# Residual stream kept with features on partitions, weights stationary in the two inner down projections, token factors by a product with ones

## The chip, the core and the metric

The kernel runs on one core of a Trainium2 chip. Its time is the device time of one execution in microseconds, the median of three runs. A profile of one more execution shows what each engine did: PE is TensorE (PEld its weight loads), DVE is VectorE, ACT is ScalarE, POOL is GpSimd, SP issues most of the transfers.

## What is computed

One decoder block on 256 tokens of 1024 features, in float32: a gated feed-forward part (FFN1), a mixing part with attention and a gated spatial branch side by side, a second feed-forward part (FFN2) and a last norm.

```python
h = h + 0.5 * swiglu(rmsnorm(h, ffn1_norm), w_gate, w_up, w_down)      # D_FF = 2816
n = rmsnorm(h, mix_norm)
z = n @ w_in                                   # q, k, v, u, gv
...
merged = gates[..., :D] * (attn @ w_branch_attn) + gates[..., D:] * (gm @ w_branch_gmlp)
h = h + merged @ w_out
h = h + 0.5 * swiglu(rmsnorm(h, ffn2_norm), ...)
return rmsnorm(h, final_norm)
```

`rmsnorm(x, g)` is `x * rsqrt(mean(x*x) + eps) * g`. The factor `rsqrt(...)` is one number for each token. It commutes with a projection, so the kernel projects `h * g` and multiplies the result by the token factor afterwards.

## The kernel before

**Products.** Every float32 operand is split into a high part, rounded to the format that TensorE takes in one pass, and a low part, the rest. A product is high·high + high·low + low·high. `by_passes` does it with the weights stationary and both parts of the activations side by side as the moving operand: one product of 512 columns (`mm_high`) and one of 256 (`mm_low`) for each block of 128x128 weights. `mm3` does it with the activations stationary and 512 columns of weights moving, in three products.

**Weights.** A unit is a piece of a weight matrix, 1 MB. It is fetched in two halves by SP's queue into seven buffers (`fetch_to`) and split in two halves into a ring of four tiles (`split_to`): ScalarE casts the high part, VectorE subtracts to get the low part, 128x1024 each. `unit(i, ahead)` splits two or three units ahead of the one that TensorE takes.

**Residual.** `h` has tokens on partitions (two groups of 128 tokens, 1024 features each). FFN1 and FFN2 have 22 blocks of 128 hidden features each. `products` makes gate and up of a block with weights stationary, `collect` adds the two halves of a PSUM bank (ScalarE copies one, VectorE adds), and `gate_up` multiplies by `rows` (the token factors, spread over all partitions by `rows_of`, which is two transposes on TensorE and a copy), then silu, a product and a split into `aT`.

`down` is the down projection with activations stationary, used three times: after FFN1 (22 blocks of 128 rows), as the output projection of the mixing part (8 blocks) and after FFN2 (22). After the first two, `done` multiplies by the norm's gain and sums the squares (`square_sum` on ScalarE, with a running sum, then `rstd_of`: two small VectorE operations and a power on GpSimd), and `put_T` turns the result by TensorE transposes, four to a bank, into `nT` with features on partitions for the next projection. The transposes stand among the products of the last two units. In FFN2 the first two blocks are made with the activations stationary (`by_tokens`) and turned afterwards.

**Order.** TensorE and SP take their instructions in the order of the code. The order on VectorE and ScalarE is a scheduler's, made when the program is built; each engine takes its list strictly in turn. PSUM has eight banks, given out in rotation.

Of the kernel before, what the change touches and what calls it, by code (L numbers as in the profile page):

```python
# [18 lines left out]
P = 128  # L19
# [24 lines left out]
def block_kernel(ctx, tc, t, out):  # L44
# [8 lines left out]
    psum = ctx.enter_context(tc.tile_pool(name="psum", bufs=8, space=PSUM))  # L53

# [4 lines left out]
    h = act.tile([P, NT, D], F32, tag="h", name="h")  # L59

    def norm_gain(ap, name):
        gb = consts.tile([P, ap.shape[-1]], F32, tag="gain", name=name)
        nc.sync.dma_start(gb, ap.to_broadcast([P, ap.shape[-1]]))
        return gb
# [4 lines left out]
    front = act.tile([P, FB * S], F32, tag="aTh", name="front")  # L69
    back = act.tile([P, ROW], F32, tag="nC", name="back")  # L70

    def load_front(queue, k, end, c0=0, c1=ROW):

        a, b = KB * (k + c0 > 0) + k * ROW + c0, KB + (end - 1) * ROW + c1
        to = back[:, c0:c1] if k == KB - 1 else front[:, a:b]
        queue.dma_start(to, t["first"][:, a:b])
# [10 lines left out]
    nc.vector.memset(eps, EPS)  # L87

# [33 lines left out]
    fetched, done_to = [2 * FIRST], [FIRST]  # L122
# [18 lines left out]

    def split_to(n):
        while done_to[0] < min(n, len(units)):
            i = done_to[0]
            done_to[0] += 1
            unit_tile(i)
            for hf in range(2):
                fetch_to(2 * i + hf + RAW)
                w, sl = parts[i], half(i, hf)
                split(w[:, sl, 0, :], w[:, sl, 1, :], raws.pop((i, hf)))  # L150
        fetch_to(2 * done_to[0] + RAW)
# [16 lines left out]
    def by_passes(sides, ks=range(KB)):  # L168


        for k in ks:
            if k < KB - 1:
# [7 lines left out]
        if KB - 1 in ks:  # L180
            for ps, of in sides:
                (sh, _), both = of(KB - 1)
                mm_high(ps, sh, both, False, True)
# [26 lines left out]
    def split(hi, lo, src):  # L210
        nc.scalar.copy(hi, src)  # L211
        nc.vector.tensor_sub(lo, src, hi.bitcast(F32))  # L212
# [19 lines left out]
    def gained(hh, gain, j, half):  # L232
        sl = slice(half * 512, half * 512 + 512)
        hg = tmp.tile([P, 512], F32, tag="hg", name=f"hg{j}{half}")
        nc.vector.tensor_mul(hg, hh[:, j, sl], gain[:, sl])
        return hg

    sums = {}

    def square_sum(hh, j, hf, name):  # L240

        if hf == 0:
            sums[name, j] = small.tile([P, 2], F32, tag="ss", name=f"ss{name}{j}")
        sq = tmp.tile([P, 512], BF16, tag="sq", name=f"sq{name}{j}{hf}", bufs=1)
        nc.scalar.activation(sq, hh[:, j, hf * 512:(hf + 1) * 512], AF.Square,
                             accum_out=sums[name, j][:, hf:hf + 1])

    def rstd_of(j, name):

        ss = sums.pop((name, j))  # L250
        ms = small.tile([P, 1], F32, tag="ms", name=f"ms{name}{j}")
        nc.vector.tensor_add(ms, ss[:, 0:1], ss[:, 1:2])
        nc.vector.tensor_scalar(ms, ms, 1.0 / D, EPS, op0=ALU.mult, op1=ALU.add)
        r = small.tile([P, 1], F32, tag="rstd", name=f"rstd{name}{j}")
        nc.gpsimd.tensor_tensor(r, ms, nhalf, op=ALU.pow)
        return r
# [20 lines left out]
    def by_tokens(name, i, nT, j):  # L277

        ps, w = bank(name), unit(i)
        tk = slice(j * P, (j + 1) * P)  # L280
        by_passes([(ps, lambda k: (tuple(p[:, tk] for p in block_of(nT, k)), w[:, k]))])
        return ps

    HALVES = ((0, 512), (512, 512))

    def down(i0, n_units, part_of, scale, hh, name, done, put=None, following=(), cuts=(HALVES, HALVES)):


# [28 lines left out]
        for j in range(NT):  # L317
            for hf, (c0, n) in enumerate(cuts[j]):
# [7 lines left out]
                if put and j == 1:  # L326
                    if hf == 0:
                        put(0, 0)
                        put(0, 1)
                    else:  # L330
                        for q in range(2):
                            put(1, q)
                            following[q]()

    def ffn_alloc(name):
        aT = (act.tile([P, FB, S], F32R, tag="aTh", name=f"{name}h"),
              act.tile([P, FB, S], F32R, tag="aTl", name=f"{name}l"))
        return aT, lambda k: (aT[0][:, k, :], aT[1][:, k, :])

    def gate_up(aT, gu, rows, name, f):  # L340
# [6 lines left out]
        split(aT[0][:, f, :], aT[1][:, f, :], a)  # L347

    def products(i0, nT, name, f):
        gu = tmp.tile([P, 2, S], F32, tag="gu", name=f"gu{name}{f}")  # L350
# [14 lines left out]
    def in_front(k, end):  # L365
        if k == KB - 1:
            return back.rearrange("p (k c) -> p k c", k=1)
# [4 lines left out]
    for k, end in zip(CUTS, CUTS[1:]):  # L372
# [24 lines left out]
        with tc.manual_schedule(engines={mybir.EngineType.DVE, mybir.EngineType.Activation}):  # L397
# [6 lines left out]
    fetch_to(2 * FIRST + RAW)  # L404
    for j in range(NT):
        nc.sync.dma_start(h[:, j, :], t["x"][j * P:(j + 1) * P, :])
    aT, aT_block = ffn_alloc("f1")
    first = act.tile([P, 4, 2, S], F32, tag="nD", name="first")
    rs = []
    for group in ((0, 1), (2,), (3,)):  # L410
        if group == (3,):
            for j in range(NT):
                for hf in range(2):
                    square_sum(h, j, hf, "1")
                rs.append(rstd_of(j, "1"))
# [11 lines left out]
    gu4 = products(f1, nT, "f1", 4)  # L427
    rows = rows_of(rs, "1")
# [23 lines left out]
    rs2 = {}  # L452

    def to_norm(nT, gain, rs, name):

        hg = {}

        def done(new, j, hf):
            hg[j, hf] = gained(new, gain, j, hf)
            square_sum(new, j, hf, name)  # L460
            if hf:
                rs[j] = rstd_of(j, name)

        return done, lambda j, hf: put_T(nT, hg.pop((j, hf)), j, hf)

# [3 lines left out]
    def value(ps, i0, j, u):  # L469
# [11 lines left out]
    gain3 = norm_gain(t["ffn2_norm"], "gain3")  # L481


    mix_a = act.tile([P, FB, S], F32, tag="aTh", name="mix_a")
# [312 lines left out]
```

## Time and profile before

| what | value |
|---|---|
| median of three runs | 538.65 us (538.56 to 539.09) |
| the profiled execution, device time | 538.97 us |
| its span (first to last instruction) | 537.2 us, so 1.8 us lie around it |
| TensorE busy | 529.5 us (99%) |
| VectorE, ScalarE busy | 389.8 us (73%), 300.3 us (56%) |
| GpSimd busy | 10.9 us (2%) |
| bytes moved | 103.02 MB, 192 GB/s on average |

The profiled execution is 0.3 us above the median. A busy TensorE is not TensorE at its peak: a product's shown duration overlaps the next one's, so costs are read from the distance between starts.

### The profile page before, as it was taken

Reading aid. Unit: us, or ns where it says so; the run is one execution under the profiler, and the core shown is the slowest. Engines: PE = TensorE matmul, PEld = TensorE weight load, DVE = VectorE, ACT = ScalarE, POOL = GpSimd, SP = SyncE. Lnnn points to the kernel's source line nnn. Section 1 sums busy time; section 2 is a strip of 40 time slices with the busy share of each in tenths; the row PEclk is TensorE's granted clock in tenths of the full one; section 3 lists DMA queues with packets and bytes.
Section 4 is the critical chain, followed back from the end, with each engine's and each line's share of the span. In section 5 each row is a group of like instructions: output and inputs, shape, how many; then the busy total and the mean of one; then the engine's idle time right before and its main releaser. Section 6 shows DMA issues by size and latency. Waiting matters only on the chain.

```text
span 537.2 us, 7918 instructions
## 1 busy us (share of the span) xinstructions
PE 529.5 (99%) x2962; PEld 459.7 (86%) x2962; DVE 389.8 (73%) x627; ACT 300.3 (56%) x534; POOL 10.9 (2%) x23
## 2 busy tenths in 40 slices
PE   8999999999999999999999999999999999999995
PEld 7888888888888888888888998888888888888884
DVE  6879988787534676968897786787787877854325
ACT  7877565565434356457886445675655656553302
POOL 0000000000000010000000000000000000000002
PEclk9999999999999999999999999999999999999998
DMA  8985765657755468564256545476546556565002
GB/s 312 418 297 187 249 220 169 210 173 246 244 196 194 159 204 266 171 212 145 84 190 201 172 140 198 141 231 221 207 164 207 181 188 204 168 206 186 30 0 78
DMA packets 29429, 103.02 MB, mean 192 GB/s; under 512 B 3408, under 2 KB 3920, under 8 KB 29392
## 3 DMA queue, kind: packets, MB, share of 16 engines
q1 hardware_dynamic: 29104, 102.20, 56.2%
q8 instruction: 23, 0.38, 0.3%
q10 hardware_dynamic: 288, 0.33, 0.2%
q14 instruction: 14, 0.11, 0.1%
HBM read 101.46 MB, written 1.05 MB: 191 GB/s over the span
## 4 chain that ended last, share of the span: by engine, by line
PE 97%; DMA 1%; DVE 0%; issue 0%; ACT 0%; POOLq 0%; DVEq 0%; POOL 0%; ACTq 0%
PE acch L199 9%; PE acch L197 9%; PE acch L198 9%; PE f2u L161 7%; PE f2g L161 7%; PE f1u L161 6%; PE f1g L161 6%; PE pgate L161 6%; PE f L161 4%; PE f2u L166 4%; PE f2g L166 4%; PE f1u L166 3%; PE f1g L166 3%; PE pgate L166 3%; PE pq L161 3%; PE f L166 2%
## 5 line engine op out<-in xcount | busy, mean ns | idle before, releaser
L212 DVE TENSOR_TENSOR w<-raw,w 128x1024 fp32r<-128x1024 f32 x180 | 217.4, 1224 | 61.2 <-ACT w L211 60.7
L211 ACT CAST w<-raw 128x1024 fp32r<-128x1024 f32 x180 | 181.7, 1056 | 68.6 <-PE acch L199 37.8
L161 PE MATMUL f2g<-n,w 128*128 128x512 f32 x160 | 62.7, 392 | 0.0
L161 PE MATMUL f2u<-n,w 128*128 128x512 f32 x160 | 62.6, 391 | 0.0
L161 PE MATMUL f1g<-n,w 128*128 128x512 f32 x144 | 56.3, 391 | 0.0
L161 PE MATMUL f1u<-n,w 128*128 128x512 f32 x144 | 56.3, 391 | 0.0
L166 PE MATMUL f2u<-n,w 128*128 128x256 f32 x160 | 39.2, 283 | 0.0
L166 PE MATMUL f2g<-n,w 128*128 128x256 f32 x160 | 39.1, 282 | 0.0
L166 PE MATMUL f1u<-n,w 128*128 128x256 f32 x144 | 35.3, 283 | 0.0
L166 PE MATMUL f1g<-n,w 128*128 128x256 f32 x144 | 35.2, 282 | 0.0
L161 PEld LDWEIGHTS f2u<-n,w 128*128 128x128 f32 x160 | 30.1, 188 | 5.7
L161 PEld LDWEIGHTS f2g<-n,w 128*128 128x128 f32 x160 | 30.1, 188 | 5.6
L197 PE MATMUL acch<-w,f1h 128*128 128x512 f32 x88 | 34.3, 390 | 0.0
L199 PE MATMUL acch<-w,f1l 128*128 128x512 f32 x88 | 34.3, 389 | 0.0
L198 PE MATMUL acch<-w,f1h 128*128 128x512 f32 x88 | 34.2, 389 | 0.0
L161 PE MATMUL pgate<-n,w 128*128 128x512 f32 x128 | 33.1, 395 | 0.0
L198 PE MATMUL acch<-w,f2h 128*128 128x512 f32 x84 | 32.7, 389 | 0.0
L199 PE MATMUL acch<-w,f2l 128*128 128x512 f32 x84 | 32.7, 389 | 0.0
L197 PE MATMUL acch<-w,f2h 128*128 128x512 f32 x84 | 32.7, 389 | 0.0
L161 PEld LDWEIGHTS f1u<-n,w 128*128 128x128 f32 x144 | 27.1, 188 | 5.1
L161 PEld LDWEIGHTS f1g<-n,w 128*128 128x128 f32 x144 | 27.1, 188 | 5.0
L166 PEld LDWEIGHTS f2u<-n,w 128*128 128x128 f32 x160 | 30.6, 191 | 0.8
(200 smaller groups left out, 992.8 us busy)
## 6 DMA issues: line engine op xcount, KB each, us to landing
raw<-in_f SPq DMA_DIRECT2D x84, 512.0 KB, 4.8
raw<-in_f1d SPq DMA_DIRECT2D x22, 512.0 KB, 4.3
raw<-in_f2d SPq DMA_DIRECT2D x22, 512.0 KB, 4.3
raw<-in_gate SPq DMA_DIRECT2D x16, 512.0 KB, 4.4
raw<-in_qk SPq DMA_DIRECT2D x8, 512.0 KB, 4.7
raw<-in_out SPq DMA_DIRECT2D x8, 512.0 KB, 4.4
front<-in_first SPq DMA_DIRECT2D x6, 384.0 KB, 6.5
raw<-in_v SPq DMA_DIRECT2D x4, 512.0 KB, 4.5
```

What stands on the lines that cost most here:

```text
L161: nc.tensor.matmul(ps, st, both.rearrange("p two n -> p (two n)"), start=first, stop=last)
L166: nc.tensor.matmul(ps[:, n:], st, both[:, 0, :], start=False, stop=False)
L197: nc.tensor.matmul(ps, sh, mh, start=first, stop=False)
L198: nc.tensor.matmul(ps, sh, ml, start=False, stop=False)
L199: nc.tensor.matmul(ps, sl, mh, start=False, stop=last)
L211: nc.scalar.copy(hi, src)
L212: nc.vector.tensor_sub(lo, src, hi.bitcast(F32))
```

## The change

`h` gets features on partitions. The two inner down projections become `down_features`: weights stationary, the hidden activations moving, one PSUM bank for each of eight blocks of 128 output features, so that the result is already turned and `put_T` is gone. Each finished bank is added to `h` by VectorE in two halves, ScalarE makes the high part with the gain as scale, and VectorE makes the low part one block later. Sums of squares are made across partitions: ScalarE squares (`square`), three adds fold eight blocks into one (`token_sums`; on GpSimd for the first norm, on VectorE for the others), the sum is split, and one product with a matrix of ones adds over partitions (`token_factors`). Four reducing operations against the identity then pick the two columns of sums out of PSUM, and GpSimd takes the power. `rows_of` for the first norm comes one block of FFN1 later, after block 5 in place of block 4. `in_order` fixes the order on VectorE and ScalarE to that of the code in three places; elsewhere it is the scheduler's still. The features are permuted in blocks of 32, and VectorE transposes of 32x32 with a trip through DRAM (`hd`, written at block 5 of FFN2 and read back at block 9 as `ht`) give the last down projection its tokens on partitions; that projection is as before. Gains come as columns. FFN2's first blocks use `products` like the others.

```diff
+    h = act.tile([P, KB, S], F32, tag="h", name="h")
...
+    def split_half(later=False):
+
+        i, hf = divmod(done_to[0], 2)
+        if hf == 0:
+            unit_tile(i)
+        fetch_to(done_to[0] + RAW)
+        done_to[0] += 1
+        w, sl = parts[i], half(i, hf)
+        return split(w[:, sl, 0, :], w[:, sl, 1, :], raws.pop((i, hf)), later)
...
-    def put_T(nT, src, j, half):
-
-        ps = bank(f"tr{j}{half}")
-        for b in range(4):
-            nc.tensor.transpose(ps[:, b * P:(b + 1) * P], src[:, b * P:(b + 1) * P], ident)
-        tk = slice(j * P, (j + 1) * P)
-        split(nT[half][:, :, 0, tk], nT[half][:, :, 1, tk], ps.rearrange("p (b t) -> p b t", b=4))
...
+    def in_order():
+        return tc.manual_schedule(engines={mybir.EngineType.DVE, mybir.EngineType.Activation})
+
+    squares = {}
+
+    def square(hh, pair, name, tag=None):
+
+        if pair == 0:
+            squares[name] = act.tile([P, KB, S], F32, tag=tag, name=f"sq{name}")
+        two = slice(2 * pair, 2 * pair + 2)
+        nc.scalar.activation(squares[name][:, two, :], hh[:, two, :], AF.Square, scale=D ** -0.5)
+
+    def token_sums(name, engine=nc.vector):
+
+        sq = squares[name]
+        for n in (4, 2, 1):
+            engine.tensor_add(sq[:, :n, :], sq[:, :n, :], sq[:, n:2 * n, :])
+        squares[name] = tmp.tile([P, 2, S], F32R, tag="hg", name=f"sqp{name}")
+        split(squares[name][:, 0, :], squares[name][:, 1, :], sq[:, 0, :])
+
+    def token_factors(name):
+
+        ps = bank(f"sums{name}")
+        nc.tensor.matmul(ps, ones, squares.pop(name).rearrange("p two n -> p (two n)"), start=True, stop=True)
+
+        ms = small.tile([P, NT], F32, tag="ms", name=f"ms{name}")
+        for j in range(NT):
+            so_far = EPS
+            for q in range(2):
+                own = tmp.tile([P, P], BF16, tag="own", name=f"own{name}{j}{q}", bufs=1)
+                to = ms[:, j:j + 1] if q else small.tile([P, 1], F32, tag="ms1", name=f"ms1{name}{j}")
+                nc.vector.tensor_tensor_reduce(own, ps[:, q * S + j * P:q * S + (j + 1) * P], ident, 1.0, so_far,
+                                               op0=ALU.mult, op1=ALU.add, accum_out=to)
+                so_far = to
+        r = small.tile([P, NT], F32, tag="rstd", name=f"rstd{name}")
+        nc.gpsimd.tensor_tensor(r, ms, nhalf.to_broadcast([P, NT]), op=ALU.pow)
+        return [r[:, j:j + 1] for j in range(NT)]
...
+    def down_features(i0, n_units, both_of_k, scale, gain, nT, name, free):
...
+        acc = [bank(f"acc{name}{c}") for c in range(KB)]
+        K = 2 * n_units
+
+        def blocks(cs, ks):
+            def of(c):
+                def at(k):
+                    w, sl = parts[i0 + k // 2], slice(c * P, (c + 1) * P)
+                    return (w[:, k % 2, 0, sl], w[:, k % 2, 1, sl]), both_of_k(k)
+                return at
+            by_passes([(acc[c], of(c)) for c in cs], ks, K)
+
+        for i in range(n_units - 2):
+            unit(i0 + i, ALONE if i == n_units - 3 else PAIRED)
+            for cs in ((range(KB - 2), range(KB - 2, KB)) if i == 0 else (range(KB),)):
+                blocks(cs, (2 * i, 2 * i + 1))
+
+        def low_part(c):
+            hi, low = block_of(nT, c)
+            nc.vector.scalar_tensor_tensor(low, h[:, c, :], gain[:, c:c + 1], hi.bitcast(F32),
+                                           op0=ALU.mult, op1=ALU.subtract)
...
+        lows = []
+        for c in range(KB):
+            blocks([c], range(K - 4, K))
+            for q in range(2):
+                nc.vector.scalar_tensor_tensor(h[:, c, :], acc[c][:, q * S:(q + 1) * S], scale, h[:, c, :],
+                                               op0=ALU.mult, op1=ALU.add)
+            nc.scalar.activation(block_of(nT, c)[0], h[:, c, :], AF.Identity, scale=gain[:, c:c + 1])
+            if c:
+                low_part(c - 1)
+            if c in (4, KB - 1):
+                lows.append(split_half(True))
+            if c % 2:
+                square(h, c // 2, name, free)
+        low_part(KB - 1)
+        for rest in lows:
+            rest()
+        token_sums(name)
...
+    fetch_to(2 * FIRST + 6)
+    for c in range(2):
+        nc.sync.dma_start(h[:, 4 * c:4 * c + 4, :],
+                          t["first"][:, KB:].rearrange("p (k c) -> p k c", k=KB)[:, 4 * c:4 * c + 4, :S])
...
-            for j in range(NT):
-                for hf in range(2):
-                    square_sum(h, j, hf, "1")
-                rs.append(rstd_of(j, "1"))
+            for pair in range(KB // 2):
+                square(h, pair, "1", "nC")
+            token_sums("1", nc.gpsimd)
...
 gu4 = products(f1, nT, "f1", 4)
+    rs = token_factors("1")
+    gu5 = products(f1, nT, "f1", 5)
     rows = rows_of(rs, "1")
     for f in range(4):
         gate_up(aT, first[:, f], rows, "f1", f)
     gate_up(aT, gu4, rows, "f1", 4)
-    ffn_blocks(f1, aT, nT, rows, "f1", range(5, FB))
-    gain2 = norm_gain(t["mix_norm"], "gain2")
-
-
-    bgate = consts.tile([P, 2 * KB], F32, name="bgate")
-    nc.sync.dma_start(bgate, t["b_gate"])
+    gate_up(aT, gu5, rows, "f1", 5)
+    ffn_blocks(f1, aT, nT, rows, "f1", range(6, FB))
...
-    done, put = to_norm(nT2, gain2, rs2, "2")
-    down(f1d, FB // 2, aT_block, 0.5, h, "h1", done, put,
-         (lambda: value(pv, mv, 0, 0), lambda: value(pv, mv, 0, 1)))
...
+    with in_order():
+        down_features(f1d, FB // 2, aT_both, 0.5, gain2, nT2, "2", "nD")
+        for u in range(2):
+            for j in range(NT):
+                value(pv, mv, j, u)
+        rs2 = token_factors("2")
...
+    with in_order():
+        down_features(mo, 4, lambda k: both_of(mT, k), 1.0, gain3, nT3, "3", "aT")
+        aT, aT_both = ffn_alloc("f2")
+
+        first = act.tile([P, 3, 2, S], F32, tag="nA", name="first2")
+        gu = [products(f2, nT3, "f2", f, first[:, f]) for f in range(2)]
+        rs = token_factors("3")
+        gu.append(products(f2, nT3, "f2", 2, first[:, 2]))
+        gu.append(products(f2, nT3, "f2", 3))
+        rows = rows_of(rs, "3")
+
+        squares32 = act.tile([P, KB, KB, 32], F32, tag="nB", name="squares32")
+        for f in range(4):
+            for b in range(2 * f, 2 * f + 2):
+                nc.vector.transpose(squares32[:, b], h[:, :, b * 32:(b + 1) * 32])
+            gate_up(aT, gu[f], rows, "f2", f)
...
+        if f == 5:
+            for a in range(4):
+                nc.sync.dma_start(hd[:, a * UC:(a + 1) * UC].rearrange("(b c) n -> c b n", c=32),
+                                  squares32[32 * a:32 * a + 32].rearrange("p b k r -> p b (k r)"))
+        elif f == 9:
+            for j in range(NT):
+                nc.sync.dma_start(ht[:, j, :], hd[j * P:(j + 1) * P, :])
```

The order of instructions at three places. On TensorE around the first norm's rows: `f1g4` and `f1u4` are gate and up of FFN1's block 4, `n` the input of the projection, `w4` and `w5` the weight units. Before:

```order
L161 MATMUL f1g4_433<-n11_115,w4_296 128x512
L161 MATMUL f1u4_434<-n11_115,w4_296 128x512
L262 MATMUL rows1_473<-ident_84,rstd10_362 128x128
L262 MATMUL rows1_473<-ident_84,rstd11_372 128x128
L161 MATMUL f1g5_523<-n10_114,w5_303 128x512
```

With the change:

```order
L162 MATMUL f1g5_491<-n11_118,w5_305 128x512
L162 MATMUL f1u5_492<-n11_118,w5_305 128x512
L270 MATMUL rows1_531<-ident_85,rstd1_479 128x128 x2
L162 MATMUL f1g6_588<-n10_117,w6_367 128x512
L162 MATMUL f1u6_589<-n10_117,w6_367 128x512
```

The two transposes of `rows_of` (`rows1`) stand one block later. The product `sums1` stands where they stood.

On ScalarE in front of them: `raw5_0` is the first half of unit 5, `sq` the squares, `lo` the copies for blocks 3 and 4, `sqp1` the folded sum of squares. Before:

```order
L211 CAST w5_303<-raw5_0_187 128x4x256
L245 ACTIVATE sq100_355,ss10_354<-h_78 128x512
L245 ACTIVATE sq101_357,ss10_354<-h_78 128x512
L245 ACTIVATE sq110_365,ss11_364<-h_78 128x512
L204 COPY lo_417<-f1_30_383 128x256
L245 ACTIVATE sq111_367,ss11_364<-h_78 128x512
L204 COPY lo_420<-f1_31_384 128x256
L211 CAST w5_303<-raw5_1_197 128x4x256
```

With the change:

```order
L238 ACTIVATE sq1_356<-h_80 128x512 x4
L212 CAST w5_305<-raw5_0_195 128x4x256
L205 COPY lo_410<-f1_30_376 128x256
L205 COPY lo_413<-f1_31_377 128x256
L212 CAST sqp1_364<-sq1_356 128x256
L212 CAST w5_305<-raw5_1_199 128x4x256
L212 CAST w6_367<-raw6_0_203 128x4x256
L212 CAST w6_367<-raw6_1_208 128x4x256
L205 COPY lo_460<-f1g4_426 128x256
```

The four squares stand together now and ahead of unit 5's first half, and the cast of `sqp1`, which needs GpSimd's adds, stands in front of the casts of units 5 and 6.

On VectorE after it: `guf14` collects block 4, `own` and `ms` are the four reducing operations (the second row of each reads its sum out), `rstd` follows the last of them. Before, behind block 4's collects:

```order
L208 TENSOR_TENSOR guf14_423<-f1g4_433,lo_467 128x256
L208 TENSOR_TENSOR guf14_423<-f1u4_434,lo_470 128x256
L212 TENSOR_TENSOR w7_424<-raw7_0_210,w7_424 128x4x256
L342 TENSOR_TENSOR first_193<-first_193,rowsb1_476 128x512
L212 TENSOR_TENSOR w7_424<-raw7_1_299,w7_424 128x4x256
L342 TENSOR_TENSOR first_193<-first_193,rowsb1_476 128x512
L346 TENSOR_TENSOR af10_481<-sgf10_479,first_193 128x256
```

With the change, behind the same collects:

```order
L214 TENSOR_TENSOR w7_417<-raw7_0_212,w7_417 128x4x256
L259 ISA own100_469,ms110_470<-sums1_466,ident_85 128x128
L259 ISA ms110_470 128x1
L214 TENSOR_TENSOR w7_417<-raw7_1_301,w7_417 128x4x256
L259 ISA own101_472,ms1_468<-sums1_466,ident_85,ms110_470 128x128
L259 ISA ms1_468 128x1
L214 TENSOR_TENSOR w8_482<-raw8_0_306,w8_482 128x4x256
L259 ISA own110_474,ms111_475<-sums1_466,ident_85 128x128
L259 ISA ms111_475 128x1
L259 ISA own111_477,ms1_468<-sums1_466,ident_85,ms111_475 128x128
L259 ISA ms1_468 128x1
L214 TENSOR_TENSOR w8_482<-raw8_1_310,w8_482 128x4x256
```

The four reducing operations stand between the subtractions of units 7 and 8; before, the factors were made ahead of block 4's collects.

## Rows read from the trace of the kernel before

**Rows 1.** the page: part 1 (busy time), part 4 (the last chain).

```profile
PE 529.5 (99%) x2962; PEld 459.7 (86%) x2962; DVE 389.8 (73%) x627; ACT 300.3 (56%) x534; POOL 10.9 (2%) x23
...
PE 97%; DMA 1%; DVE 0%; issue 0%; ACT 0%; POOLq 0%; DVEq 0%; POOL 0%; ACTq 0%
```

**Rows 2.** TensorE timeline (start, us, instruction): FFN1, its down projection.

```profile
99.98 0.40 PE L161 MATMUL f1g<-n,w 128*128 128x512 f32 x1
...
105.54 0.40 PE L161 MATMUL f1g<-n,w 128*128 128x512 f32 x1
...
128.28 0.39 PE L197 MATMUL acch<-w,f1h 128*128 128x512 f32 x1
...
185.41 1.03 PE L228 MATMUL tr<-ident,hg 128*128 128x128 f32 x8
186.20 0.48 PE L197 MATMUL acch<-w,f1h 128*128 128x512 f32 x1
186.52 0.39 PE L198 MATMUL acch<-w,f1h 128*128 128x512 f32 x1
...
188.81 0.39 PE L199 MATMUL acch<-w,f1l 128*128 128x512 f32 x1
189.04 0.60 PE L228 MATMUL tr<-ident,hg 128*128 128x128 f32 x4
189.40 0.48 PE L197 MATMUL pv<-w,n 128*128 128x512 f32 x1
```

**Rows 3.** VectorE and ScalarE by line and shape (count | busy us, mean ns).

```profile
L298 DVE SCALAR_TENSOR_TENSOR h<-endh,h 128x256 f32<-128x256 f32 x2 | 0.8, 417 | 0.5 <-PE endh L199 0.5
L386 DVE SCALAR_TENSOR_TENSOR n<-front,n 128x256 fp32r<-128x256 f32 x7 | 3.4, 481 | 1.0 <-ACT n L381 1.0
...
L381 ACT ACTIVATE n<-front 128x256 fp32r<-128x256 f32 x7 | 3.6, 510 | 2.7 <-DMA front<-in_first 2.6
```

**Rows 4.** the timeline of ScalarE before the first norm's sums of squares are ready.

```profile
23.72 1.06 ACT L211 CAST w<-raw 128x1024 fp32r<-128x1024 f32 x1
...
25.43 0.63 ACT L245 ACTIVATE sq<-h 128x512 bf16<-128x512 f32 x1
25.97 0.19 ACT L245 ACTIVATION_READ_ACCUMULATOR sq<-h 128x1 f32 x1
```

**Rows 5.** DMA issues: KB each, median us from issue to landing.

```profile
h<-in_x SPq DMA_DIRECT2D x2, 512.0 KB, 10.9
```

**Rows 6.** GpSimd's groups by line and shape.

```profile
L255 POOL TENSOR_TENSOR rstd<-ms,nhalf 128x1 f32<-128x1 f32 x6 | 4.2, 703 | 214.1 <-DVE ms L253 214.1
...
L727 POOL TENSOR_TENSOR o<-o,rstd 128x512 f32<-128x512 f32 x1 | 1.0, 1043 | 0.1
```

**Rows 7.** VectorE and GpSimd together, timeline at the second norm's factors.

```profile
193.24 1.22 DVE L212 TENSOR_TENSOR w<-raw,w 128x1024 fp32r<-128x1024 f32 x1
...
193.40 1.47 POOL L255 TENSOR_TENSOR rstd<-ms,nhalf 128x1 f32<-128x1 f32 x1 [7.99 <-DVE ms L253]
```

**Rows 8.** VectorE: three weight subtractions; the reducing operation by shape.

```profile
30.04 3.50 DVE L212 TENSOR_TENSOR w<-raw,w 128x1024 fp32r<-128x1024 f32 x3 [0.53 <-ACT w L211]
...
L712 DVE CUSTOM_DVE_ANT_0 sq<-h,ms 128x512 bf16<-128x512 f32 x1 | 0.8, 751 | 0.2 <-DVE h L298 0.2
L712 DVE CUSTOM_DVE_ANT_0 sq<-h,ms 128x256 bf16<-128x256 f32 x1 | 0.5, 484 | 0.1
```

**Rows 9.** TensorE after FFN1 block 5: the first product of block 6.

```profile
39.21 0.39 PE L161 MATMUL f1g<-n,w 128*128 128x512 f32 x1
```

**Rows 10.** TensorE's warm-up products at the start.

```profile
1.18 3.32 PE L95 MATMUL warm<-zeros 128*128 128x256 bf16 x16 [1.18 <-DVE zeros L92]
```

**Rows 11.** windows (busy us by engine, granted clock, DMA share): end, FFN2.

```profile
531.00:533.00 2.00, 0.14 (x2) 0.00 (x0) 1.25 (x4) 0.00 (x0) 0.81 (x2) 1.00 0.08 28
...
534.00:536.00 2.00, 0.00 (x0) 0.00 (x0) 0.00 (x0) 0.00 (x0) 0.00 (x0) 0.50 0.72 262
...
370.00:500.00 130.00, 130.00 (x710) 113.26 (x710) 93.43 (x143) 71.67 (x124) 0.00 (x0) 1.00 0.57 190
```

More of the change, by code (lines that the diff above doesn't have):

```diff
@@ L140, in fetch_to @@
             nc.sync.dma_start(raws[i, hf], t[name][u][:, half(i, hf), :])
-    def split_to(n):
[L143 to L146, printed above, removed]
-            for hf in range(2):
[L148 to L151, printed above, removed]
+    def split_half(later=False):
[6 more added lines that the diff above has]
+        return split(w[:, sl, 0, :], w[:, sl, 1, :], raws.pop((i, hf)), later)
+    def split_to(n):
+        while done_to[0] < 2 * min(n, len(units)):
+            split_half()
+        fetch_to(done_to[0] + RAW)
     def unit(i, ahead=PAIRED):
@@ L275, in by_weights, with down @@
         return ps
[L277 to L282, printed above, removed]
-    HALVES = ((0, 512), (512, 512))
-    def down(i0, n_units, part_of, scale, hh, name, done, put=None, following=(), cuts=(HALVES, HALVES)):
+    HALVES = ((0, 512), (512, 512))
+    def down_features(i0, n_units, both_of_k, scale, gain, nT, name, free):
[33 more added lines that the diff above has]
+        token_sums(name)
+    def down(i0, n_units, part_of, scale, hh, name, done, cuts):
         acc = {(j, c0): bank(f"acc{name}{j}{c0}") for j in range(NT) for c0, n in HALVES}
@@ L325, in down @@
                 done(hh, j, hf)
[L326 to L333, printed above, removed]
     def ffn_alloc(name):
-        aT = (act.tile([P, FB, S], F32R, tag="aTh", name=f"{name}h"),
-              act.tile([P, FB, S], F32R, tag="aTl", name=f"{name}l"))
-        return aT, lambda k: (aT[0][:, k, :], aT[1][:, k, :])
+        aT = act.tile([P, FB, 2, S], F32R, tag="aT", name=f"{name}h")
+        return aT, lambda k: aT[:, k]
     def gate_up(aT, gu, rows, name, f):
@@ L680, in block_kernel @@
-    aT, aT_block = ffn_alloc("f2")
-    for i in range(2):
-        first_columns(1, i)
-    rows = rows_of(rs3, "3")
-    a0 = []
-    for j in range(NT):
-        s = tmp.tile([P, UC], F32, tag="s", name=f"s{j}")
-        nc.scalar.activation(s, gu0[j][:, 0, :], AF.Silu, scale=rs3[j])
-        a0.append(tmp.tile([P, UC], F32, tag="us", name=f"a0{j}"))
-        nc.vector.scalar_tensor_tensor(a0[j], gu0[j][:, 1, :], rs3[j], s, op0=ALU.mult, op1=ALU.mult)
-    ffn_blocks(f2, aT, nT3, rows, "f2", [2])
@@ L691, in block_kernel @@
-    for j in range(NT):
-        pt = bank(f"f2t{j}")
-        for b in range(2):
-            nc.tensor.transpose(pt[:, b * P:(b + 1) * P], a0[j][:, b * P:(b + 1) * P], ident)
-        tk = slice(j * P, (j + 1) * P)
-        split(aT[0][:, 0:2, tk], aT[1][:, 0:2, tk], pt[:, :UC].rearrange("p (b t) -> p b t", b=2))
-    ffn_blocks(f2, aT, nT3, rows, "f2", range(3, FB))
+    with in_order():
+        down_features(mo, 4, lambda k: both_of(mT, k), 1.0, gain3, nT3, "3", "aT")
[11 more added lines that the diff above has]
+            gate_up(aT, gu[f], rows, "f2", f)
@@ new lines, in block_kernel @@
+    hd = dram.tile([S, D], F32, name="hd")
+    ht = act.tile([P, NT, D], F32, tag="nA", name="ht")
+    for f in range(4, FB):
+        ffn_blocks(f2, aT, nT3, rows, "f2", [f])
+        if f == 5:
[3 more added lines that the diff above has]
+        elif f == 9:
+            for j in range(NT):
+                nc.sync.dma_start(ht[:, j, :], hd[j * P:(j + 1) * P, :])
+        elif f == 12:
+            gain4 = act.tile([P, D], F32, tag="nB", name="gain4")
+            nc.sync.dma_start(gain4, t["final_norm"].to_broadcast([P, D]))
@@ L736, in done3 @@
                 nc.sync.dma_start(out[rows, a:b], y[:, a:b])
[L738 removed]
+    down(f2d, FB // 2, lambda k: (aT[:, k, 0, :], aT[:, k, 1, :]), 0.5, ht, "h3", done3, last_cuts)
 def _packed(inputs):
```

141 lines of the change are left out of this document (47 added, 94 removed).

## The prediction

> **What bounds the kernel now.** I read the page first: TensorE is busy for 99% of the span, and the chain that ended last is TensorE for 97% [rows 1]. So no other engine's saving is worth anything by itself. What counts is how long TensorE's own queue of products is, and whether something new makes it wait. The page's busy time can't price a product, since shown durations overlap (a 512-column product lasts 0.39 us or more and the next starts earlier), so the timeline of TensorE comes second, read by the distance between starts. One FFN1 block, 16 products of 512 columns and 16 of 256, takes 105.54 - 99.98 = 5.56 us [rows 2], that is 0.348 for a pair of 512 and 256. The first down projection runs from 128.28 to 189.04 [rows 2]; without the eight transposes inside it (0.79) and the slow product behind them (0.09 more than its like) its 264 products take 59.9 us, 0.227 each. A 256-column product is then worth 0.348 - 0.227 = 0.12. TensorE does not wait at the two places that the change rebuilds: the transposes stand directly behind products and the next products directly behind them.
>
> **TensorE's own work.** The two inner down projections have 30 row blocks. Before: 30 x 12 = 360 products of 512 columns, 360 x 0.227 = 81.7 us. With the change: 30 x 8 = 240 pairs, 240 x 0.348 = 83.5 us. That is the same number of columns in more instructions, +1.8 us. Three products with ones at 0.23 add 0.7. What goes are 16 transposes for each of two norms, 0.79 for eight and 0.36 for four and for four again [rows 2], 1.5 each, and the four that turned FFN2's first blocks, 0.36: 3.4 us. The first product behind each of these seven runs takes 0.32 in place of 0.23 [rows 2], 0.6 in all. The sum is +2.5 - 4.0 = -1.5 us. FFN2's first blocks have the same products either way.
>
> **What is hidden at the second and third norm.** In the last stretch TensorE gives a feature block four pairs, 4 x 0.348 = 1.39 us. VectorE does two accumulations at 0.42 and one low part at 0.48 for it [rows 3], 1.3 us, so it keeps up. Behind the last block it needs 0.9 for the accumulations, ScalarE 0.5 for the high part [rows 3], VectorE 0.5 for the low part: 1.9 us. At the second norm the first 24 products of the value projection use only blocks 0 to 3 and cover 24 x 0.227 = 5.4 us; in FFN2 block 7 is asked for after 12 products of 512 columns and more, also over 2.7 us. The factors follow by two weight subtractions of 1.2 [rows 8], three adds (under 2.3 by the same width), a split (0.9), four more subtractions, four reducing operations with one or two subtractions between, and the power: some 19 us, and `rows_of` asks for them after 22 (eight half units of the two value projections, 96 products; or four blocks of 5.56). I cost both at nothing; the cover left is about 3 us, and each us beyond it would cost one. The eight accumulators need all banks; the last two are asked for 12 pairs, 4.2 us, after the first, and a collect takes under 1.
>
> **The trip through DRAM.** Eight VectorE transposes of 256 columns aren't in the trace. From below they cost like a 256-wide operation, 0.42 [rows 3], from above like a 1024-wide one, 1.17 [rows 8]: 3.4 to 9.4 us on an engine that is idle for 36 of 130 us in FFN2 [rows 11]. I take 4: the operand is 256 wide. Nothing on TensorE asks for it before the backlog is some 4 us deeper, and only the upper bound reaches that (1 us at most). The transfers, 2 MB more on queues that are 57% busy there [rows 11], have tens of us to spare. SP's wait for the transposes holds weight fetches behind it, which run seven halves ahead; cost 0.
>
> **The first norm is where I expect the loss.** Follow the order shown above. ScalarE starts the squares at 23.72, where unit 5's cast stood [rows 4]. Squares follow each other at 25.97 - 25.43 = 0.54, so the four end at 25.9. The residual is there: its transfers landed 10.9 us after issue [rows 5] and now leave one fetch earlier. Then GpSimd folds 1792 columns. It took 1.04 us for 512 [rows 6], so 3.6, to 29.5. During this VectorE wants to subtract unit 5's first half (1.2 us). In the one place of the trace where a GpSimd operation and such a subtraction meet, the power took 1.47 [rows 7]; the six powers sum to 4.2 [rows 6], so the other five took 0.55. A subtraction that has begun thus seems to hold GpSimd off. I take that: 30.7 (without it 29.5).
>
> The Trainium skill, SBUF — State Buffer, section Who interferes with whom, states this as a rule: a VectorE instruction with two SBUF inputs and a GpSimd instruction that reads SBUF exclude each other for a whole instruction. The rows agree in that one case; by the rule the adds end at 30.7, without it at 29.5.
>
> ScalarE's cast of the folded sum (256 wide, 0.5) and VectorE's subtraction (0.4) bring 31.6. The product with ones is asked for at 33.4 and finds its input. But VectorE, strictly in turn, has four collects (0.42 each, 1.7), six weight subtractions (three take 3.50 [rows 8], so 7.0) and the four reducing operations before the power. These are 128 wide; 484 ns at 256 and 751 at 512 [rows 8] give 0.35, with 0.08 to read the sum 0.43, together 1.7. That is 10.4 us: the last one ends at 42.0. The next subtraction follows at once, as in [rows 7], so the power takes 1.5: 43.5. TensorE has finished block 5 at 39.2 (block 6's first product started then [rows 9], and the product with ones takes the place of the two transposes). So it stands for **4.3 us** in front of the two transposes, with everything behind them. Without any exclusion it is 40.8 + 0.55 = 41.4, 2.2 us. From above, if two full operands halve GpSimd's rate, 3.6 more: 7.9.
>
> A gap of that length also touches the clock. The 16 warm-up products of 256 columns took 3.3 us at the start [rows 10], 0.2 each against 0.12 later: for about 3 us TensorE ran at the lower of its two levels, 1.2 GHz. After the last product the granted clock was still 1.00 in the window to 533 and 0.50 in the window from 534 [rows 11], so it fell within 3 us of idleness. I therefore expect it to fall in this gap and to come back after some 3 us of products, which costs half of that, **1.5 us** (0 if it doesn't fall).
>
> The Trainium skill, TensorE: Matmul & The Clock Gate, section HAM oscillation, warns that idle gaps between bursts of matmuls put the clock back to half rate each time. The rows at the end of the kernel agree; by the rule the 1.5 us are due, and without it the time would be 541.4.
>
> **Sum.** -1.5 + 4.3 + 1.5 = +4.3 us on the profiled execution's 538.97, 543.3. That execution is 0.3 above the median, so for the median 542.9.
>
> **Rivals.**
> First, the factors come in time and only TensorE's own work changes: -1.5, 537.1. For it: the factors are asked for one block later than before, 5.6 us. Against it: VectorE's 10.4 us behind the folded sum; even if GpSimd took nothing, the cast stands behind ScalarE's two copies of block 3, which TensorE ends at 39.2 - 2 x 5.56 = 28.1; with 0.8 for them, 0.9 for cast and split, 10.4 and 0.55 the power ends near 40.7, after 39.2. It decides if the last reducing operation ends before 38.6. Chance 0.08.
> Second, a short stop, 2.2 us or less, without a fall of the clock: -1.5 + 2.2 = +0.7, 539.3. For it: no exclusion is seen on a long GpSimd operation. Chance 0.14.
> Third, the forecast's family, a stop of 2.2 to 4.3 with or without the fall: 540.8 to 542.9. Chance 0.64, most of it at the upper end.
> Fourth, more: GpSimd's adds at half the rate (-1.5 + 7.9 + 1.5, 546.5), or the 3 us of cover at the later norms don't hold because in-order VectorE waits for ScalarE in turn. Chance 0.14.
>
> The measurement can tell about 0.2% (1.1 us) from no change. Faster by more: the first rival, 0.08. Within: the second, 0.14. Slower: 0.78. The range from 538.9 (it leaves out the first rival and part of the second) to 546.0 (it leaves out half of the fourth).
>
> **What would show it.** Right: in the profile after, TensorE's first idle gap of over 1 us stands in front of `rows1` near 39 us and ends with GpSimd's power; the granted clock falls there and returns; the down projections are longer by 1.4 and 0.4 us; no transposes behind them, and no gap in front of the second and third `rows_of`. Wrong: `rows1` without a wait (then the list on VectorE runs faster than its rows say, or GpSimd does), a wait at the value projection or at FFN2's first block (then the low parts come late), or starts of the 256-column products with other distances than 0.12.

## The result: 545.53 us, 1.3% slower

The changed kernel takes 545.53 us (median of 4 runs, 545.49 to 545.57), the kernel before 538.69 (538.56 to 539.09, 4 runs). The ratio is 1.0126, with a 95% interval from 1.0108 to 1.0143. The profiled execution took 545.57 us with a span of 543.5, so 2.1 us lie around it; before, 538.97, 537.2 and 1.8.

The page of the changed kernel, its busy times and the chain that ended last, beside [rows 1]:

```profile
PE 531.2 (98%) x3049; PEld 464.9 (86%) x3049; DVE 405.6 (75%) x682; ACT 302.7 (56%) x534; POOL 17.4 (3%) x23
...
PE 93%; DVE 2%; POOL 1%; ACT 1%; issue 1%; DMA 1%; POOLq 0%; DVEq 0%; ACTq 0%
```

TensorE is busy only 1.7 us longer, but it holds 93% of the chain in place of 97%: for some microseconds the chain now runs through VectorE, GpSimd and ScalarE. What TensorE waited for in the whole span (total, times, longest, in us) says where:

```profile
PE rows L270 <- POOL rstd L263: 4.3, 1, 4.3
...
```

This is the new wait, for GpSimd's power, in front of the first norm's two transposes. TensorE's timeline there and at later landmarks:

```profile
38.97 0.40 PE L162 MATMUL f1u<-n,w 128*128 128x512 f32 x1
43.63 0.69 PE L270 MATMUL rows<-ident,rstd 128*128 128x128 f32 x2 [4.27 <-POOL rstd L263]
43.97 0.78 PE L162 MATMUL f1g<-n,w 128*128 128x512 f32 x1
44.55 0.63 PE L162 MATMUL f1u<-n,w 128*128 128x512 f32 x1
44.97 0.63 PE L162 MATMUL f1g<-n,w 128*128 128x512 f32 x1
...
135.81 0.39 PE L162 MATMUL acc<-f1h,w 128*128 128x512 f32 x1
...
196.90 0.39 PE L162 MATMUL acc<-f1h,w 128*128 128x512 f32 x1
197.13 0.39 PE L198 MATMUL pv<-w,n 128*128 128x512 f32 x1
...
219.15 0.38 PE L270 MATMUL rows<-ident,rstd 128*128 128x128 f32 x2
...
376.40 0.39 PE L270 MATMUL rows<-ident,rstd 128*128 128x128 f32 x2
```

Block 6 starts at 43.97 in place of 39.21 [rows 9], 4.76 us late. Its first products follow each other at 0.43 us (44.97 - 44.55) in place of 0.23. The down projection (the first `acc` line) starts at 135.81 in place of 128.28 [rows 2], 7.53 us late, so 2.77 more were lost in FFN1 behind the wait. From there to the end of the span it is 543.5 - 135.81 = 407.7 us in place of 537.2 - 128.28 = 408.9: 1.2 us are won back. The value projection follows the down projection at 0.23 (196.90 to 197.13), and the second and third transposes stand without a wait.

The windows around the wait (busy us of PE, PEld, DVE, ACT, POOL, then the granted clock, the DMA share, GB/s) show why the products behind it are slow:

```profile
39.40:42.80 3.40, 0.00 (x0) 0.00 (x0) 3.36 (x9) 1.36 (x3) 0.85 (x1) 1.00 0.93 313
42.90:49.60 6.70, 5.97 (x15) 4.78 (x16) 5.61 (x14) 3.47 (x8) 0.68 (x1) 0.50 0.57 217
49.80:52.00 2.20, 2.20 (x19) 2.15 (x18) 0.07 (x1) 0.00 (x0) 0.00 (x0) 1.00 0.00 0
```

TensorE idled through the first window and the clock still stood at its upper level, 2.4 GHz. Shortly before the wait ended it fell to 1.2 GHz, and it stayed there for 6 us of products.

What made the factors late is on GpSimd and VectorE. GpSimd's timeline (three adds in one row, then the power of the first norm; the powers of the second and third):

```profile
26.01 5.46 POOL L244 TENSOR_TENSOR sq<-sq 128x1024 f32<-128x1024 f32 x3 [24.28 <-ACT sq L238]
41.95 1.62 POOL L263 TENSOR_TENSOR rstd<-ms,nhalf 128x2 f32<-128x2 f32 x1 [10.48 <-DVE ms L259]
...
214.37 1.62 POOL L263 TENSOR_TENSOR rstd<-ms,nhalf 128x2 f32<-128x2 f32 x1 [69.53 <-DVE ms L259]
...
371.70 1.61 POOL L263 TENSOR_TENSOR rstd<-ms,nhalf 128x2 f32<-128x2 f32 x1 [143.99 <-DVE ms L259]
```

VectorE's timeline from unit 5's first half to the last of the four reducing operations:

```profile
26.90 2.61 DVE L214 TENSOR_TENSOR w<-raw,w 128x1024 fp32r<-128x1024 f32 x1 [1.73 <-ACT w L212]
31.95 0.43 DVE L214 TENSOR_TENSOR sqp<-sq,sqp 128x256 fp32r<-128x256 f32 x1 [2.44 <-ACT sqp L212]
...
37.31 1.21 DVE L214 TENSOR_TENSOR w<-raw,w 128x1024 fp32r<-128x1024 f32 x1
38.44 0.28 DVE L259 CUSTOM_DVE_ANT_0 own<-sums,ident 128x128 bf16<-128x128 f32 x1
...
38.65 1.22 DVE L214 TENSOR_TENSOR w<-raw,w 128x1024 fp32r<-128x1024 f32 x1
...
41.52 0.35 DVE L259 CUSTOM_DVE_ANT_0 own<-sums,ident,ms 128x128 bf16<-128x128 f32 x1
41.79 0.08 DVE L259 DVE_READ_ACCUMULATOR2_ANT ms<- 128x1 f32 x1
```

The reader should see two delays in a row. First VectorE stands idle until 31.95, because the fold of the squares comes from GpSimd at 31.5. Then its list runs on with one gap of 0.2 us: collects, six weight subtractions and the reducing operations, which end at 41.87. Three of the subtractions stand between or just ahead of the reducing operations (37.31, 38.65 and one at 40.05).

### The profile page after: what moved, and what is told of

It reads as the page before. It is cut to its first block, busy times and chain, and to the rows that moved or that the text cites. A ratio compares the mean times of both kernels' runs of the same rounds, so it can differ in the third digit from the quotient of the medians.

```text
span 543.5 us, 8142 instructions
## 1 busy us (share of the span) xinstructions
PE 531.2 (98%) x3049; PEld 464.9 (86%) x3049; DVE 405.6 (75%) x682; ACT 302.7 (56%) x534; POOL 17.4 (3%) x23
## 4 chain that ended last, share of the span: by engine, by line
PE 93%; DVE 2%; POOL 1%; ACT 1%; issue 1%; DMA 1%; POOLq 0%; DVEq 0%; ACTq 0%
PE acc L162 10%; PE f2u L162 7%; PE f2g L162 7%; PE f1g L162 6%; PE f1u L162 6%; PE pgate L162 5%; PE acc L167 5%; PE f2u L167 4%; PE f2g L167 4%; PE acch L200 4%; PE acch L199 4%; PE acch L198 3%; PE f1u L167 3%; PE f1g L167 3%; PE pgate L167 3%; PE pq L162 3%
## 5 line engine op out<-in xcount | busy, mean ns | idle before, releaser
L162 PE MATMUL f2g<-n,w 128*128 128x512 f32 x176 | 68.8, 391 | 0.0
L162 PE MATMUL f2u<-n,w 128*128 128x512 f32 x176 | 68.8, 391 | 0.0
L162 PE MATMUL f1g<-n,w 128*128 128x512 f32 x144 | 58.0, 403 | 0.0
L162 PE MATMUL acc<-f1h,w 128*128 128x512 f32 x176 | 43.4, 391 | 0.0
L167 PE MATMUL f2u<-n,w 128*128 128x256 f32 x176 | 43.2, 283 | 0.0
L167 PE MATMUL f2g<-n,w 128*128 128x256 f32 x176 | 43.0, 282 | 0.0
L162 PEld LDWEIGHTS f2u<-n,w 128*128 128x128 f32 x176 | 33.1, 188 | 6.3
L162 PEld LDWEIGHTS f2g<-n,w 128*128 128x128 f32 x176 | 33.1, 188 | 6.1
L162 PEld LDWEIGHTS acc<-f1h,w 128*128 128x128 f32 x176 | 31.9, 188 | 5.8
L167 PEld LDWEIGHTS f2u<-n,w 128*128 128x128 f32 x176 | 33.7, 191 | 0.8
L167 PEld LDWEIGHTS f2g<-n,w 128*128 128x128 f32 x176 | 33.6, 191 | 0.9
L199 PE MATMUL acch<-w,f2h 128*128 128x512 f32 x84 | 32.7, 389 | 0.0
L200 PE MATMUL acch<-w,f2h 128*128 128x512 f32 x84 | 32.7, 389 | 0.0
L198 PE MATMUL acch<-w,f2h 128*128 128x512 f32 x84 | 32.7, 389 | 0.0
```

The costliest lines, as they stand in the source:

```text
L162: nc.tensor.matmul(ps, st, both.rearrange("p two n -> p (two n)"), start=first, stop=last)
L167: nc.tensor.matmul(ps[:, n:], st, both[:, 0, :], start=False, stop=False)
L198: nc.tensor.matmul(ps, sh, mh, start=first, stop=False)
L199: nc.tensor.matmul(ps, sh, ml, start=False, stop=False)
L200: nc.tensor.matmul(ps, sl, mh, start=False, stop=last)
```

## The experiments

The theory was the one of the prediction: the loss is TensorE's wait for the first norm's factors and the lower clock behind it, and the rest of the change gains a little. The rivals: that the later blocks are slow for another reason than the clock, that the rest of the change costs something too, and that one of GpSimd and VectorE alone makes the factors late. Every time is a median of at least 5 runs, beside the kernel before on the same chip (538.80 for the first four, 538.77 for the last two). The changed kernel's 545.53 is the result above, beside 538.69 for the kernel before, so a difference of 0.1 us from it says nothing.

**The rows one block later.**

```diff
-    gu4 = products(f1, nT, "f1", 4)
+    gu4 = products(f1, nT, "f1", 4, act.tile([P, 2, S], F32, tag="early", name="early"))
     rs = token_factors("1")
     gu5 = products(f1, nT, "f1", 5)
+    gu6 = products(f1, nT, "f1", 6)
     rows = rows_of(rs, "1")
...
-    ffn_blocks(f1, aT, nT, rows, "f1", range(6, FB))
+    gate_up(aT, gu6, rows, "f1", 6)
+    ffn_blocks(f1, aT, nT, rows, "f1", range(7, FB))
```

> The changed kernel with the first norm's token factors asked for one FFN1 block later, after block 6 in place of block 5 (one more tile keeps block 4's sums). Theory (the loss is TensorE's wait for the factors and the lower clock behind it): the power ends near 43.6, TensorE asks at 39.2 + 5.56 = 44.8, so there is no wait and the granted clock stays 1.00; 4.4 us of wait and 3.0 us of slow products go, 545.5 - 7.4 = 538.1 (537.8 to 538.5). Rival (VectorE's backlog, which the later factors make 5.6 us longer, comes back as a wait further on, in FFN1 or at the down projection's start): 540 or more, with a gap of TensorE elsewhere.

It took 537.60 us, ratio to the kernel before 0.998 (0.9971 to 0.9989). GpSimd's power stands at 41.92, as late as in the changed kernel, and TensorE asks for it only after it has ended. GpSimd's and TensorE's timelines:

```profile
41.92 1.62 POOL L263 TENSOR_TENSOR rstd<-ms,nhalf 128x2 f32<-128x2 f32 x1 [10.48 <-DVE ms L259]
```

```profile
44.73 0.38 PE L270 MATMUL rows<-ident,rstd 128*128 128x128 f32 x2
44.87 0.48 PE L162 MATMUL f1g<-n,w 128*128 128x512 f32 x1
...
128.47 0.39 PE L162 MATMUL acc<-f1h,w 128*128 128x512 f32 x1
```

The wait is gone, no other took its place, and the down projection starts 7.3 us earlier than in the changed kernel. So the wait and what follows from it are the whole loss, and the backlog on VectorE did not come back. From 128.47 to the span's end at 535.8 it is 407.3 us, against 408.9 before.

**The same wait, filled.**

```diff
     gu5 = products(f1, nT, "f1", 5)
+    fill = bank("fill")
+    for i in range(36):
+        nc.tensor.matmul(fill[:, :S], zeros[:, :P], zeros, start=True, stop=True)
     rows = rows_of(rs, "1")
```

> The changed kernel with 36 products of 256 columns of zeros (0.107 each, 3.9 us; the result is used nowhere) between block 5 and the two transposes of the first norm, so that TensorE waits as long but is not idle. Theory (the products behind the wait are slow because the clock fell in it): block 6 still starts near 44.0, the granted clock stays 1.00, products of 512 columns follow each other at 0.227 at once, 545.5 - 3.0 = 542.5. Rival (they are slow because weights or buffers come late behind the wait): spacing stays near 0.43 and the time at 545.5.

It took 542.08 us, 3.45 less than the changed kernel (some 0.3 of it outside the span: about 1.7 us lie around it here, 2.1 there). TensorE's timeline and windows:

```profile
39.38 4.10 PE L467 MATMUL fill<-zeros 128*128 128x256 bf16 x36
43.81 0.43 PE L270 MATMUL rows<-ident,rstd 128*128 128x128 f32 x2 [0.33 <-POOL rstd L263]
44.00 0.48 PE L162 MATMUL f1g<-n,w 128*128 128x512 f32 x1
...
133.19 0.39 PE L162 MATMUL acc<-f1h,w 128*128 128x512 f32 x1
```

```profile
39.40:43.70 4.30, 4.08 (x37) 3.41 (x36) 4.26 (x11) 2.58 (x4) 1.56 (x1) 1.00 0.94 308
44.00:49.70 5.70, 5.70 (x35) 5.01 (x35) 5.70 (x10) 2.68 (x7) 0.00 (x0) 1.00 0.97 358
```

Block 6 starts at the same time as in the changed kernel (44.00 against 43.97), so the wait is untouched; the clock stays at 1.00, and from block 6 to the down projection it takes 89.19 us in place of 135.81 - 43.97 = 91.84. Weights and buffers behind the wait were in time. The clock's fall costs 2.65 us there, and 0.15 more at the two transposes (0.34 us to the next product in the changed kernel, 0.19 here): 2.8 in all.

**The first norm as before, the rest changed.**

```diff
+    xt = act.tile([P, NT, D], F32, tag="nC", name="xt")
+    for j in range(NT):
+        nc.sync.dma_start(xt[:, j, :], t["x"][j * P:(j + 1) * P, :])
...
-            for pair in range(KB // 2):
-                square(h, pair, "1", "nC")
-            token_sums("1", nc.gpsimd)
+            rs = []
+            for j in range(NT):
+                ss = small.tile([P, 2], F32, tag="ss0", name=f"ss1{j}")
+                for hf in range(2):
...
+                    nc.scalar.activation(sq, xt[:, j, hf * 512:(hf + 1) * 512], AF.Square,
+                                         accum_out=ss[:, hf:hf + 1])
...
+                nc.gpsimd.tensor_tensor(r1, ms1, nhalf, op=ALU.pow)
...
-    rs = token_factors("1")
-    gu5 = products(f1, nT, "f1", 5)
     rows = rows_of(rs, "1")
```

> The changed kernel with the first norm's factors made as before the change (its own copy of the input with tokens on partitions, squares with a running sum on ScalarE, two small operations on VectorE, power on GpSimd for each group of tokens, factors asked for after block 4); the rest as changed. Theory (the whole loss comes from the first norm, and the rest of the change gains 1.3 us in the span and loses 0.3 outside it): no wait of TensorE at the first norm, 538.7 - 1.3 + 0.3 - 0.2 (no product with ones) = 537.5 (537.2 to 538.1). Rival (the rest of the change costs something too, or the extra copy of the input, 1 MB, delays the first weights): 538.7 or more.

It took 537.44 us, ratio 0.9974 (0.9965 to 0.9983). TensorE came to the transposes after block 4, without a wait (GpSimd's second power ended at 27.6):

```profile
33.25 0.38 PE L270 MATMUL rows<-ident,rstd 128*128 128x128 f32 x2
...
128.13 0.39 PE L162 MATMUL acc<-f1h,w 128*128 128x512 f32 x1
```

The rest of the change thus gains 1.4 us in all; what its single parts cost or gain is not shown. This is the fastest version of the study, level with the first within their spread (537.27 to 537.90, against 537.52 to 538.01).

**The reducing operations ahead of units 7 and 8.** `products` gets a parameter `ahead`, which says how many units are split ahead.

```diff
-    gu4 = products(f1, nT, "f1", 4)
-    rs = token_factors("1")
-    gu5 = products(f1, nT, "f1", 5)
+    with in_order():
+        gu4 = products(f1, nT, "f1", 4, ahead=ALONE - 1)
+        rs = token_factors("1")
+        gu5 = products(f1, nT, "f1", 5)
```

> The changed kernel with the order on VectorE and ScalarE written out at the first norm: the four reducing operations follow block 4's two collects directly, and the four weight subtractions of units 7 and 8, of which three stood ahead of the last reducing operation, come behind them. GpSimd's three adds stay. Theory (the factors are late by VectorE's list): collects end at 37.4, reducing operations at 38.9, the power takes up to 1.6, to 40.4; TensorE waits 1.2 us in place of 4.4 and the clock does not fall: 545.5 - 3.2 - 3.0 = 539.3 (539.0 to 539.8; 542.3 if the clock falls all the same). Rival (GpSimd's adds, not the list, make them late, or the later subtractions make units 7 and 8 late): 542 or more, with a wait for a weight unit.

It took 539.03 us, ratio to the kernel before 1.0005 (0.9997 to 1.0014). The end of VectorE's last reducing operation, GpSimd's adds and power, TensorE's transposes, and a window around the wait:

```profile
38.65 0.08 DVE L259 DVE_READ_ACCUMULATOR2_ANT ms<- 128x1 f32 x1
```

```profile
26.04 5.46 POOL L244 TENSOR_TENSOR sq<-sq 128x1024 f32<-128x1024 f32 x3 [24.31 <-ACT sq L238]
38.82 1.62 POOL L263 TENSOR_TENSOR rstd<-ms,nhalf 128x2 f32<-128x2 f32 x1 [7.32 <-DVE ms L259]
```

```profile
40.49 0.43 PE L270 MATMUL rows<-ident,rstd 128*128 128x128 f32 x2 [1.11 <-POOL rstd L263]
40.68 0.48 PE L162 MATMUL f1g<-n,w 128*128 128x512 f32 x1
```

```profile
39.20:44.00 4.80, 3.69 (x18) 2.91 (x18) 4.80 (x7) 2.91 (x5) 1.24 (x1) 1.00 0.72 241
```

With GpSimd's adds as slow as ever the power comes 3.1 us earlier, and the wait shrinks to 1.1 us. Over this gap the granted clock stayed at 1.00. The order, without faster adds, is worth 6.5 us, most of it in the wait (block 6 starts 3.3 us earlier) and the slow products behind it. The edit writes out ScalarE's order too, but that list stays as it was until block 5's copies, so the gain comes from VectorE's.

**The adds on VectorE.**

```diff
-            token_sums("1", nc.gpsimd)
+            token_sums("1")
```

> The changed kernel with the first norm's three adds on VectorE in place of GpSimd; the scheduler's order otherwise. It tells GpSimd's share from that of VectorE's list. Theory (the list decides): the adds end near 29.3 in place of 31.5 and unit 5's first subtraction takes 1.2 in place of 2.6, but the three adds and seven weight subtractions still stand ahead of the last reducing operation, which also stands behind block 5's first collect; it ends near 41.5 and the power between 42.1 and 43.1. TensorE waits 2.9 to 3.9 us in place of 4.4: 544.0 to 545.0 with the clock's fall, 541 to 542 without it. Rival (GpSimd's slow adds are the whole cause): the factors come before 39.2 and the time is near 538.

It took 542.01 us, ratio to the kernel before 1.0053 (1.0039 to 1.0066): less than expected with the clock's fall, and the rival did not come true either. VectorE, GpSimd and TensorE, and TensorE's windows:

```profile
25.97 1.95 DVE L244 TENSOR_TENSOR sq<-sq 128x1024 f32<-128x1024 f32 x2 [0.80 <-ACT sq L238]
27.84 1.22 DVE L214 TENSOR_TENSOR w<-raw,w 128x1024 fp32r<-128x1024 f32 x1
28.97 0.42 DVE L244 TENSOR_TENSOR sq<-sq 128x256 f32<-128x256 f32 x1
...
40.96 0.09 DVE L259 DVE_READ_ACCUMULATOR2_ANT ms<- 128x1 f32 x1
40.96 0.42 DVE L209 TENSOR_TENSOR guf<-f1u,lo 128x256 f32<-128x256 f32 x1
```

```profile
41.13 0.71 POOL L263 TENSOR_TENSOR rstd<-ms,nhalf 128x2 f32<-128x2 f32 x1 [39.41 <-DVE ms L259]
```

```profile
41.89 0.43 PE L270 MATMUL rows<-ident,rstd 128*128 128x128 f32 x2 [2.52 <-POOL rstd L263]
42.08 0.48 PE L162 MATMUL f1g<-n,w 128*128 128x512 f32 x1
...
132.84 0.39 PE L162 MATMUL acc<-f1h,w 128*128 128x512 f32 x1
```

```profile
41.90:43.00 1.10, 1.10 (x6) 0.97 (x7) 0.85 (x2) 0.37 (x1) 0.00 (x0) 1.00 0.97 268
43.50:46.40 2.90, 2.90 (x9) 2.22 (x8) 2.90 (x7) 2.26 (x6) 0.00 (x0) 0.50 0.93 364
```

The adds take 2.4 us in place of 5.46 and unit 5's subtraction 1.22 in place of 2.61, but the list behind them still ends at 41.05, only 0.8 us earlier. The expectation erred at two places. TensorE waited 2.52 us where 2.9 to 3.9 were expected: the list ended at 41.05 and not near 41.5, and the power, for which 0.6 to 1.6 were allowed, took 0.71 (a 256-wide collect that reads PSUM stands behind the last reducing operation here, not a weight subtraction). And the clock's fall cost less: the products ran at 1.2 GHz for about 3 us in place of 6, which made block 6 to the down projection 132.84 - 42.08 = 90.76 us, 1.6 more than without a fall (89.19).

**Both together.** The edits of the last two runs in one kernel.

> The kernel with block 4's collects and the four reducing operations ahead of units 7 and 8 (the run before, 539.03 us), and the first norm's three adds on VectorE as well. Theory (GpSimd's adds and VectorE's list share the lateness, and no later place for the rows is needed): folded sum split at 31.7, collects end near 35.3, reducing operations near 36.8, the power by 38.4, 0.8 us ahead of TensorE at 39.2: no wait, 537.6 (537.3 to 538.0), as with the rows one block later. Rival (taking VectorE for the adds delays unit 5 and 6's subtractions as much as the adds gain): a wait of about 1 us stays, 538.7 to 539.2.

It took 537.83 us, ratio to the kernel before 0.998 (0.9971 to 0.9989). GpSimd's power ended at 38.5, and TensorE came later than that:

```profile
36.88 1.62 POOL L263 TENSOR_TENSOR rstd<-ms,nhalf 128x2 f32<-128x2 f32 x1 [35.16 <-DVE ms L259]
```

```profile
39.79 0.38 PE L270 MATMUL rows<-ident,rstd 128*128 128x128 f32 x2
39.92 0.48 PE L162 MATMUL f1g<-n,w 128*128 128x512 f32 x1
```

So the factors can be ready at the place where the change asks for them. Neither edit alone does it: GpSimd's adds and the weight subtractions share the lateness.

## Why the prediction was right, and what it mis-sized

The direction, the place and the mechanism were right; the time, 542.9 us, was 2.6 too low, inside the range up to 546.0. Term by term:

**The wait.** Each step of the forecast chain stands in the trace: squares to 25.9, the folded sum split at 31.6 (measured 32.4), last reducing operation 42.0 (41.9), power 43.5 (43.6), TensorE ready at 39.2 (39.4). The wait was 4.27 us where 4.3 were predicted. That it fits so closely is in part luck: two errors cancelled in it. GpSimd's adds took 5.46 us in place of 4.8. What the prediction allowed for the subtraction beside them came about (the add of 512 columns took 2.15 us, 1.1 above the 1.04 of [rows 6]; 1.2 was allowed), but the adds of 1024 and 256 columns took 2.41 and 0.74 where the price by width gives 2.08 and 0.52. VectorE's list took 9.5 us in place of 10.4: the prediction added shown durations, and on VectorE, as on TensorE, the next operation starts before the shown end (the subtraction at 37.31 lasts 1.21, and the next operation starts at 38.44, not at 38.52). Block 6 came 4.6 us late without the 0.15 that the lower clock took at the transposes, because the first product with ones (0.23), which the prediction counts as TensorE's own work, also lies ahead of it. The runs with the rows later, with the other order and with the first norm as before show that this wait and the clock are the whole loss.

**The clock: the term that failed.** The prediction expected it "to come back after some 3 us of products, which costs half of that, 1.5 us". That it fell was right. But the size came from one stretch, the warm-up products [rows 10]; here TensorE worked at 1.2 GHz for 6 us, and the run with the filled wait prices that at 2.8 us. In the run with the adds on VectorE it was about 3 us and 1.6. With 2.8 in place of 1.5 the same sum gives 544.2. The reading of the warm-up was weak as well. It rests on the spacing of the products alone, 0.2 us against 0.12 later; the profile's window of that stretch in the kernel before shows the granted clock at 1.00, so no trace shows the return from which the 3 us were taken:

```profile
0.00:3.00 3.00, 1.82 (x9) 1.32 (x10) 0.25 (x3) 1.49 (x2) 1.10 (x8) 1.00 0.35 56
```

Why the clock came back after 6 us in one run and after about 3 in another stays open.

**TensorE's own work.** Predicted -1.5. The stretch from the down projection to the end is 1.2 us shorter in the profiled execution of the changed kernel and 1.6 in that of the run with the rows later; with the first product with ones, which lies ahead of it, that is -1.0 and -1.4. The run with the first norm as before, which lacks that product, is 1.4 faster than the kernel before. So the trade of 360 products of 512 columns against 240 pairs, and of 36 transposes that go, was priced from distances between starts to within 0.5 us: the first down projection takes 197.13 - 135.81 = 61.3 us, and 176 pairs at 0.348 are 61.2.

**What was costed at nothing.** No wait at the value projection, at FFN2's first block or at the second and third transposes. The powers there end at 214.37 + 1.62 = 216.0 and 371.70 + 1.61 = 373.3, and TensorE asks at 219.15 and 376.40: 3.2 and 3.1 us of cover, as the prediction had it (about 3). The prediction's "some 19 us" for the path to the second norm's factors is what was measured (216.0 - 196.90 = 19.1), but the terms that it names add up to only 17 or 18. The trip through DRAM shows no wait of TensorE, and VectorE's eight transposes of 256 columns lasted 0.42 us each, the lower bound.

**Outside the span.** The forecast assumed no difference there. 2.0 to 2.1 us lie outside in the changed kernel and in the run with the adds on VectorE alone, 1.9 in the runs with the written order and with the old first norm, and 1.7 in the kernel before and in the other two. It is steady within each kernel; what sets it stays open. The sum for the profiled execution was 543.3, and 545.57 is 2.3 more: 0.1 for the wait, 1.3 for the clock, 0.5 for TensorE's own work in that execution and 0.3 outside the span make 2.2. One price among the prediction's rivals is loose: the third's lower end, 540.8, belongs to a stop of 2.2 us with the clock's fall; without the fall it would be 539.3, as in the second.

## What to carry to other kernels

When a kernel is bound by TensorE for 99% of its span, a change of its products is worth what the distances between starts say, here some 1.4 us, and every new dependency in front of TensorE must be followed through the lists of the in-order engines: three weight subtractions that nobody needed yet, put between four small reducing operations, cost more than the whole change could gain. Ask for a small result one stage later, or put its last steps ahead of the bulk work on their engine; the first brought this kernel from 1.3% slower to 0.2% faster, the second to level, and to 0.2% faster once the adds were quicker too. A wait of a few microseconds on TensorE has to be priced with the slow products behind it, and how long they last must not be taken from a single place of the trace.

## What the runs showed of the hardware that was not expected

- The granted clock fell after TensorE had gone back to work: in the run with the adds on VectorE it had idled 2.52 us, worked again from 41.89 at 1.00 (window 41.90 to 43.00), and ran at 0.50 in the window from 43.50. After 1.11 us of idleness (the other order) it did not fall.
- The time at 1.2 GHz differed between gaps of the same kernel family: 6 us of products behind a gap of 4.27 us, about 3 behind 2.52. Products of zeros in the same gap kept the clock at 1.00.
- GpSimd and VectorE can hold each other up, in either direction. A weight subtraction of 1.22 us took 2.61 beside GpSimd's adds; the power of two columns took 1.62 beside such a subtraction and 0.71 beside a 256-wide add that reads one operand from PSUM. The Trainium skill, SBUF — State Buffer, section Who interferes with whom, states that a VectorE instruction with both inputs in SBUF contends with a GpSimd instruction that reads SBUF; these three rows agree with it, and the prediction was right to reckon with it (43.5 in place of 41.4 for the power's end). But it does not hold everywhere: behind the third norm's reducing operations two subtractions follow each other from 371.54, the power runs from 371.70 to 373.31 beside both, and the two take 2.36 us, as two take without a power (2.35). The power did not hold up the second one; why stays open.
